# Two edits in a four-layer kernel: the order of the 64-row products in `pair_heads`, and the buffers of the gate tiles

## Chip, cores and metric

The kernel runs on one core of a Trainium2 chip. The metric is device time in microseconds (us). Before the change it is 3857.72 us, the median of 3 runs (3853.47 to 3861.3).

## What is computed

The input x has 2048 rows of 1024 fp32 values. Four layers follow one another; each projects its input with a wide weight matrix, mixes rows in two or three ways, gates the result, projects it back with a second matrix, adds the input and normalises. Layers 2 and 3 are the two that the first edit touches. Layer 2 has gated linear attention with 4 heads, 64 key channels and 128 value channels each, in chunks; layer 3 has retention of the same sizes in chunks of 128 rows. Cut to what matters, retention is

```python
scores = jnp.einsum('bnihd,bnjhd->bnhij', q, k) * dmat          # causal, inside a chunk
o_intra = jnp.einsum('bnhij,bnjhe->bnihe', scores, v)
chunk_state = jnp.einsum('bnjhd,hj,bnjhe->bnhde', k, w_state, v)
s_in = _chunk_scan(chunk_decay, chunk_state)                     # state entering each chunk
o_inter = jnp.einsum('bnihd,hi,bnhde->bnihe', q, w_inter, s_in)
return (o_intra + o_inter).reshape(B, S, H, dv)
```

and gated linear attention has the same five steps with a decay for each key channel in place of the fixed one. In all four layers part of the mixed values is multiplied by a gate of the form `h * sigmoid(h)` of one slice of the input projection.

## The kernel before

The 2048 rows are worked on in 4 blocks of 512; blocks go through the layers in pairs. In a block and layer the work is: the input projection, weight tile by weight tile (`in_a`, `in_b`, `in_b4`), with the mixing between the tiles; the gate (`gate_mix`); the output projection (`out_proj`). Every projection is done with both operands split into a high and a low part, three products for one, accumulated in one of four PSUM banks named `acc`. A second pool of four PSUM banks, `mm`, serves all other products and transposes. Each weight tile (512 KB) is loaded by a DMA on SyncE's queue into one of two buffers `wst`, rounded by ScalarE into `whi` (line 444) and its remainder taken by VectorE into `wlo` (line 313).

The source states the work in one order; a planner in the language's tile framework then places each instruction on its engine by readiness and rank, where rank follows the order in the source and `high_priority` raises it. So the order found in the trace need not be that of the source. The helpers record all work at a few lines: products at 322 (`mmul`), transposes at 325 (`tr`), VectorE products at 310 and 313, ScalarE at 299. The profile must therefore be read by tiles: `acc` for projections, `mm<-u` for the scores (key times query), `mm<-vb,t` for the state increments (transposed key times value), `mm<-vb,am` for masked scores times value, `mm<-t,u` for query times state.

`pair_heads` (line 1169) handles two heads of 64 key channels at once: head 0 lies on partitions 0 to 63, head 1 on 64 to 127. It is called twice, once for each pair of heads, in each block of layers 2 and 3. In the four chunks t of a block it forms

- the scores, for head 0 all four chunks, then for head 1: products over 64 rows;
- the masks (`masked`, VectorE, into the constant tiles `am`), the transposes of the keys (`trans4`) and the increments, products over 128 rows that write 64 partitions each;
- the states, on VectorE (`state_chain` in layer 2, lines 1188 to 1193 in layer 3);
- the outputs, head by head and chunk by chunk: a product over 128 rows (masked scores times value) that begins a sum, then one over 64 rows (query times state) that ends it;
- `finish` for each head: `rms_to_mix` (layer 2) or `groupnorm_to_mix` (layer 3).

In layer 2 the two calls are made from a hook after the first and the second weight tile of an `in_a`; in layer 3 they follow each other directly, and the four projections of the pool branch come next. A product of fp32 operands appears in the trace as two matmul instructions.

`gate_mix` (line 773) ends the input projection of every layer and block, 16 times in all. For each of four row tiles ScalarE computes tanh from an accumulator into a tile `g`, VectorE multiplies it with the accumulator, which is then free, and GpSimd multiplies the tile into `mix`. `g` comes from a tag with two buffers (line 254); `u` is a tag with 13 buffers of the same size, from which norm parameters, input loads and many temporary tiles come.

Of the kernel before, what the change touches and what calls it, by code (L numbers as in the profile page):

```python
# [226 lines left out]
class Build:  # L227
# [544 lines left out]

    def gate_mix(self, accs, c0, n=512, half=None):
        for t in range(4):
            g = self.g((128, n))
            self.gate(accs[t][:, 0:n], g, 0.5 if half is None else half[:, t:t + 1])
            m = self.mix[:, t * 1024 + c0:t * 1024 + c0 + n]
            self.tt(m, m, g, ALU.mult, self.nc.gpsimd)
# [389 lines left out]

    def pair_heads(self, g, qd, kd, S, em, finish, coef=None):

        ams = []
        for i in range(2):
            r = slice(64 * i, 64 * i + 64)
            ps = self.mm()
            for t in range(4):
                c = slice(t * 128, t * 128 + 128)
                self.mmul(ps[:, c], kd[r, c], qd[r, c])
            ams.append(self.masked(ps))
        kT = self.trans4(kd)
        inc = self.mm()  # L1180
        for t in range(4):
            for i in range(2):
                self.mmul(inc[64 * i:64 * i + 64, t * 128:t * 128 + 128], kT[:, t * 128 + 64 * i:t * 128 + 64 * i + 64], self.vb[:, t, 2 * g + i, 0:128])
        if coef is None:
            Ss = self.state_chain(S, inc, em)
        else:
            Ss, iv = self.t(), self.t()
            self.nc.vector.tensor_copy(Ss[:, 0:128], S)
            self.act(iv, inc, AF.Copy, scale=coef)
            for t in range(4):  # L1190
                c = slice(t * 128, t * 128 + 128)
                dst = Ss[:, t * 128 + 128:t * 128 + 256] if t < 3 else S
                self.stt(dst, Ss[:, c], coef, iv[:, c], ALU.mult, ALU.add)
        for i in range(2):
            r = slice(64 * i, 64 * i + 64)
            o = self.mm()
            for t in range(4):
                c = slice(t * 128, t * 128 + 128)
                self.mmul(o[:, c], ams[i][:, c], self.vb[:, t, 2 * g + i, 0:128], start=True, stop=False)
                self.mmul(o[:, c], qd[r, c], Ss[r, c], start=False, stop=True)  # L1200
            finish(o, 2 * g + i)


    def ret_tables(self, b, C, S):
# [546 lines left out]
```

## Time and profile before

| | before |
|---|---|
| median of 3 runs | 3857.72 us (3853.47 to 3861.3) |
| profiled execution | 3849.46 us, span 3847.7 us |
| granted TensorE clock, mean | 0.996 |
| TensorE busy | 3740.3 us, 97% |
| VectorE busy | 2755.3 us, 72% |
| ScalarE busy | 1774.8 us, 46% |
| GpSimd busy | 586.0 us, 15% |
| HBM read, written | 378.82 MB, 58.72 MB: 114 GB/s over the span |

A row of the profile gives the line, the engine, the operation, the tile written and the tiles read, the partitions and elements of a product (64*128 is 64 rows by 128 columns of weights) and a count; in brackets stands how long the engine was idle just before and what ended that. In the chain of waits, each piece is a start, a length and what filled it. TensorE's instructions are pipelined, so their durations overlap; what one costs is read from the distance between starts.

### The profile page before, as it was taken

What the parts mean: (1) busy time and instruction counts of PE and PEld (TensorE: products, weight loads), DVE (VectorE), ACT (ScalarE), POOL (GpSimd) and SP (SyncE); (2) the same over time, 40 slices, a digit from 0 to 9 for tenths busy, and PEclk for the clock granted to TensorE, in tenths of its full rate; (3) what the DMA queues carried; (4) which work ended last, traced back from release to release, by engine and by line L of the source; (5) the groups of instructions that cost most, each with busy time, mean ns of one, the idle gap of its engine ahead of it and who ended that gap; (6) DMA issues with size and microseconds to landing.
All of it is one profiled execution on the core that took longest, in us unless ns stands there. A gap on an engine that the chain in (4) does not pass through costs nothing.

```text
span 3847.7 us, 54577 instructions
## 1 busy us (share of the span) xinstructions
PE 3740.3 (97%) x20576; PEld 3119.7 (81%) x20576; DVE 2755.3 (72%) x5807; ACT 1774.8 (46%) x3273; POOL 586.0 (15%) x445
## 2 busy tenths in 40 slices
PE   8999999999999999999999999999999999999999
PEld 7788788878787878888787887888887878888887
DVE  7776765667666798598677767656676767985985
ACT  6547343434242454355374573434333424653552
POOL 0110112112121201100301101121131211012003
PEclk9999999999999999999999999999999999999999
DMA  3332343433343332321423332434343433223212
GB/s 128 123 126 92 111 143 119 154 109 133 131 148 120 122 109 66 126 88 66 135 81 127 121 120 77 144 130 149 115 150 113 148 115 127 77 72 131 88 61 88
DMA packets 141528, 441.09 MB, mean 115 GB/s; under 512 B 15696, under 2 KB 15824, under 8 KB 141264
## 3 DMA queue, kind: packets, MB, share of 16 engines
q1 hardware_dynamic: 141264, 437.60, 33.5%
q8 instruction: 162, 2.65, 0.3%
q14 instruction: 102, 0.84, 0.1%
HBM read 378.82 MB, written 58.72 MB: 114 GB/s over the span
## 4 chain that ended last, share of the span: by engine, by line
PE 75%; DVE 13%; ACT 4%; DMA 3%; issue 2%; POOL 2%; SPq 0%; ACTq 0%; POOLq 0%; DVEq 0%
PE acc L322 61%; PE mm L322 10%; PE mm L325 4%; DVE wlo L313 3%; DMA wst<-in_wi_dram 3%; DVE u L310 2%; DVE t L313 1%; ACT whi L444 1%; POOL mix L313 1%; ACT t L299 1%; DVE t L310 1%; POOL u L313 0%; DVE g L310 0%; DVE mix L310 0%; DVE big L310 0%
## 5 line engine op out<-in xcount | busy, mean ns | idle before, releaser
L322 PE MATMUL acc<-whi,ah 128*128 128x512 f32 (+3 forms) x3072 | 1174.9, 382 | 31.3 <-DVE g L310 15.0
L322 PE MATMUL acc<-wlo,ah 128*128 128x512 f32 (+3 forms) x3072 | 1164.1, 379 | 0.0
L322 PE MATMUL acc<-whi,al 128*128 128x512 f32 (+3 forms) x3072 | 1162.1, 378 | 0.0
L313 DVE TENSOR_TENSOR wlo<-wst,whi 128x1024 fp32r<-128x1024 f32 (+2 forms) x560 | 732.0, 1308 | 475.2 <-ACT whi L444 453.7
L444 ACT CAST whi<-wst 128x1024 fp32r<-128x1024 f32 (+2 forms) x560 | 573.9, 1025 | 965.9 <-PE acc L322 609.9
L322 PE MATMUL acc<-ah,whi 128*128 128x512 f32 (+1 forms) x2048 | 709.8, 347 | 9.1 <-ACT whi L444 9.1
L322 PEld LDWEIGHTS acc<-whi,ah 128*128 128x128 f32 x3072 | 579.3, 189 | 152.6 <-DVE g L310 23.1
L322 PE MATMUL acc<-ah,wlo 128*128 128x512 f32 (+1 forms) x2048 | 697.2, 340 | 0.5 <-DVE wlo L313 0.5
L322 PE MATMUL acc<-al,whi 128*128 128x512 f32 (+1 forms) x2048 | 697.0, 340 | 0.0
L322 PEld LDWEIGHTS acc<-whi,al 128*128 128x128 f32 x3072 | 578.9, 189 | 112.4
L322 PEld LDWEIGHTS acc<-wlo,ah 128*128 128x128 f32 x3072 | 579.9, 189 | 107.9 <-issue 1.0
L322 PEld LDWEIGHTS acc<-ah,whi 128*128 128x128 f32 x2048 | 387.1, 189 | 49.9 <-ACT whi L444 9.1
L322 PEld LDWEIGHTS acc<-ah,wlo 128*128 128x128 f32 x2048 | 386.5, 189 | 42.1 <-issue 1.4
L322 PEld LDWEIGHTS acc<-al,whi 128*128 128x128 f32 x2048 | 387.2, 189 | 41.2 <-issue 2.9
L313 POOL TENSOR_TENSOR big<-big,u 128x512 f32<-128x512 f32 x96 | 139.9, 1489 | 580.3 <-PE mm L325 236.7
L313 POOL TENSOR_TENSOR mix<-mix,g 128x512 f32<-128x512 f32 x88 | 115.5, 1324 | 588.0 <-DVE g L310 520.0
L310 DVE SCALAR_TENSOR_TENSOR u<-mix,hdw,u 128x512 f32<-128x512 f32 x240 | 170.7, 746 | 0.3
L538 ACT CAST ah<-u 128x512 fp32r<-128x512 f32 x128 | 79.2, 619 | 179.7 <-PE acc L322 167.6
L310 DVE SCALAR_TENSOR_TENSOR big<-big,acc 128x512 f32<-128x512 f32 x128 | 87.5, 683 | 77.8 <-PE acc L322 77.5
L313 POOL TENSOR_TENSOR u<-u,lc 128x512 f32<-128x512 f32 (+1 forms) x64 | 76.3, 1198 | 349.1 <-DVE u L319 172.0
L322 PE MATMUL mm<-t,u 64*128 64x128 f32 (+2 forms) x480 | 101.3, 308 | 14.5 <-DVE t L313 12.8
L310 DVE SCALAR_TENSOR_TENSOR g<-g,acc 128x512 f32<-128x512 f32 x112 | 76.0, 684 | 46.1 <-ACT g L299 46.1
(345 smaller groups left out, 4801.1 us busy)
## 6 DMA issues: line engine op xcount, KB each, us to landing
wst<-in_wi_dram SPq DMA_DIRECT2D x400, 512.0 KB, 3.3
wst<-in_wo_dram SPq DMA_DIRECT2D x128, 512.0 KB, 3.3
rows<-big SPq DMA_DIRECT2D x48, 512.0 KB, 2.7
chn<-t SPq DMA_DIRECT2D x96, 256.0 KB, 4.1
u<-chn SPq DMA_DIRECT2D x96, 256.0 KB, 4.8
big<-rows SPq DMA_DIRECT2D x48, 512.0 KB, 5.6
u<-in_lnp_dram SPq DMA_DIRECT2D x48, 256.0 KB, 5.2
u<-in_xt_dram SPq DMA_DIRECT2D x32, 256.0 KB, 4.2
```

What stands on the lines that cost most here:

```text
L299: return self.nc.scalar.activation(out, in_, f, bias=bias, scale=scale)
L310: return self.nc.vector.scalar_tensor_tensor(out, in0, s, in1, op0, op1)
L313: return (eng or self.nc.vector).tensor_tensor(out, a, b, op)
L322: return self.nc.tensor.matmul(out, lhsT, rhs, start=start, stop=stop)
L325: return self.nc.tensor.transpose(out, in_, self.ident)
L444: nc.scalar.copy(hi, st)
L538: nc.scalar.copy(h, c4(st))
```

## The change

The first edit is in `pair_heads`. The scores of both heads are formed together, chunk by chunk, head 0 and head 1 in turn, into two PSUM banks. The outputs of both heads are collected in two banks at once: first all products over 128 rows, then all products over 64 rows, again chunk by chunk with the heads in turn. Since the four chunks of a head share a bank and their sums are now open together, only the first product of a bank is marked as its start, and only the last as its end. `finish` is called for both heads after all products. The second edit is in `gate_mix`: the tiles of the third and fourth row tile come from `u` instead of `g`.

```diff
     def gate_mix(self, accs, c0, n=512, half=None):
         for t in range(4):
-            g = self.g((128, n))
+            g = self.g((128, n)) if t < 2 else self.u((128, n))
...
     def pair_heads(self, g, qd, kd, S, em, finish, coef=None):
 
-        ams = []
-        for i in range(2):
-            r = slice(64 * i, 64 * i + 64)
-            ps = self.mm()
-            for t in range(4):
-                c = slice(t * 128, t * 128 + 128)
+        rows = [slice(0, 64), slice(64, 128)]
+        pss = [self.mm() for _ in range(2)]
+
+        for t in range(4):
+            c = slice(t * 128, t * 128 + 128)
+            for ps, r in zip(pss, rows):
                 self.mmul(ps[:, c], kd[r, c], qd[r, c])
-            ams.append(self.masked(ps))
+        ams = [self.masked(ps) for ps in pss]
...
+        os = [self.mm() for _ in range(2)]
         for i in range(2):
-            r = slice(64 * i, 64 * i + 64)
-            o = self.mm()
             for t in range(4):
                 c = slice(t * 128, t * 128 + 128)
-                self.mmul(o[:, c], ams[i][:, c], self.vb[:, t, 2 * g + i, 0:128], start=True, stop=False)
-                self.mmul(o[:, c], qd[r, c], Ss[r, c], start=False, stop=True)
-            finish(o, 2 * g + i)
+                self.mmul(os[i][:, c], ams[i][:, c], self.vb[:, t, 2 * g + i, 0:128], start=(t == 0), stop=False)
+        for t in range(4):
+            c = slice(t * 128, t * 128 + 128)
+            for o, r in zip(os, rows):
+                self.mmul(o[:, c], qd[r, c], Ss[r, c], start=False, stop=(t == 3))
+        for i in range(2):
+            finish(os[i], 2 * g + i)
```

## Prediction

> **What bounds the kernel now.** I read the page first: busy time, then the chain of waits.
>
> ```profile
> span 3847.7 us, 54577 instructions
> PE 3740.3 (97%) x20576; PEld 3119.7 (81%) x20576; DVE 2755.3 (72%) x5807; ACT 1774.8 (46%) x3273; POOL 586.0 (15%) x445
> PE 75%; DVE 13%; ACT 4%; DMA 3%; issue 2%; POOL 2%; SPq 0%; ACTq 0%; POOLq 0%; DVEq 0%
> ```
>
> TensorE is the bound nearly everywhere: 97% busy, 75% of the chain. A busy TensorE need not be one at its peak, though, so the question is how densely its products stand where the change works. For that I took the chain of waits through the two calls of `pair_heads` in one block of layer 3 (970 to 1030 us).
>
> ```profile
> 981.22 1.64 PE mm L322 x16
> ...
> 984.36 8.32 PE mm L322 x64
> ...
> 995.40 6.67 PE mm L322 x44
> ...
> 1002.31 0.42 PE mm L322 x4
> 1002.73 24.92 PE acc L322 x106
> ```
>
> Every piece here is TensorE, so a microsecond taken from its products in this stage comes off the end, as long as nothing else becomes late. How they stand is seen in the timeline of TensorE (start, duration, shape, count). Each fp32 product of 128 columns is two matmul instructions, so a call has 16 for the scores (`mm<-u`, 64 rows), 16 for the state increments (`mm<-vb,t`), 16 for the masked scores times v (`mm<-vb,am`, 128 rows) and 16 for q times state (`mm<-t,u`, 64 rows).
>
> ```profile
> 981.15 1.71 PE L322 MATMUL mm<-u 64*128 64x128 f32 x16
> 982.79 0.66 PE L325 MATMUL mm<-ident,u 128*128 128x128 f32 x4
> ...
> 984.29 1.09 PE L322 MATMUL mm<-vb,t 128*64 128x128 f32 x16
> 985.32 0.49 PE L322 MATMUL mm<-vb,am 128*128 128x128 f32 x2
> 985.74 0.48 PE L322 MATMUL mm<-t,u 64*128 64x128 f32 x2
> 986.15 0.71 PE L322 MATMUL mm<-vb,am 128*128 128x128 f32 x4
> 986.79 0.49 PE L322 MATMUL mm<-t,u 64*128 64x128 f32 x2
> ```
>
> Two instructions of one shape take 0.42 us from their start to the start of the other shape (985.32 to 985.74, 985.74 to 986.15); four take 0.64 (986.15 to 986.79). So each further instruction of the same shape costs 0.11, and a change of shape costs 0.42 - 2 x 0.11 = 0.20. The present order changes shape after every product. A second view shows two halves of the partitions meeting, at the end of the first call: its last product reads rows 64 to 127, the next call's scores begin on rows 0 to 63.
>
> ```profile
> 990.55 0.49 PE L322 MATMUL mm<-vb,am 128*128 128x128 f32 x2
> 990.97 0.37 PE L322 MATMUL mm<-t,u 64*128 64x128 f32 x1
> 990.97 0.37 PE L322 MATMUL mm<-u 64*128 64x128 f32 x1
> 991.18 0.27 PE L322 MATMUL mm<-t,u 64*128 64x128 f32 x1
> 991.19 1.50 PE L322 MATMUL mm<-u 64*128 64x128 f32 x15
> 992.61 0.51 PE L322 MATMUL acc<-al,whi 128*128 128x512 f32 x1
> ```
>
> The two start together at 990.97 and go on together at 991.18 and 991.19: products on different halves overlap fully.
>
> **The change part by part.** No product, copy or DMA is added or removed. Calls: the groups of instructions by shape give the count, and 256 / 16 = 16 calls (2 groups, 2 layers, 4 blocks).
>
> ```profile
> L322 PE MATMUL mm<-t,u 64*128 64x128 f32 x256 | 54.5, 322 | 0.0
> ```
>
> *128-row and 64-row products apart.* Before, in this call: 985.32 to 990.97 for 30 of the 32, 5.65 us, and 0.1 for the last two, which overlap the next call: 5.75. In layer 2 products of the input projection stand between, and the chain shows the same density, 0.188 us for one instruction:
>
> ```profile
> 568.21 3.75 PE mm L322 x20
> ```
>
> ```profile
> 566.51 0.56 DVE L313 TENSOR_TENSOR t<-t,em 128x384 f32<-128x384 f32 x1
> ```
>
> I take 5.8 for both. After: 16 of 128 rows in one stretch are 0.42 + 14 x 0.11 = 1.96; 16 of 64 rows, eight on each half side by side, are 0.42 + 6 x 0.11 = 1.08. Together 3.04, so 2.75 is saved in a call of layer 3. In layer 2 the states of the last three chunks come from one VectorE product (566.51 to 567.07, the row above) and the first chunk's earlier, so the 64-row stretch will break once: 0.2 more, 2.55 saved.
>
> *Scores alternating.* Before, 981.15 to 982.79: 1.64 us. They already overlap in part: 16 in series would be 0.42 + 14 x 0.11 = 1.96. After, as above, 1.08: 0.56 saved. That alternation in this very pattern keeps both halves going is borne out by the increments, which alternate halves of the columns: 984.29 to 985.32 is 1.03 us for 16. If the halves did not overlap at all, the scores would lose 0.32 and q times state would be 1.96, so a call gains 5.8 - 3.92 - 0.32 = 1.56, 25 us over 16 calls. This is the lower end, and 8 x (2.75 + 0.56) + 8 x (2.55 + 0.56) = 51 us is what I take, since the row at 990.97 is the same operation. Without any break in layer 2 it is 53, the upper end.
>
> *Both results at the end of a call.* The normalisation of the first head used to begin while the second head's products ran; now both begin after the last product. In layer 3 VectorE is in order, and behind the normalisation stand the masks of the second call, for which its 128-row products wait.
>
> ```profile
> 989.82 0.89 DVE L1293 BATCH_NORM_STATS2 st<-mm 128x6 f32<-128x128 f32 x4 [2.08 <-PE mm L322]
> ...
> 997.91 1.36 DVE L319 TENSOR_SCALAR mix<-mm,mv,y 128x128 f32<-128x128 f32 x4
> ```
>
> ```profile
> 981.00:1002.70 21.70, 21.70 (x152) 16.41 (x151) 13.46 (x58) 4.08 (x6) 0.00 (x0) 1.00 0.12 37
> 1002.70:1028.00 25.30, 25.30 (x111) 20.20 (x109) 24.72 (x76) 6.70 (x9) 7.15 (x4) 1.00 0.28 91
> ```
>
> These are the two windows' busy times (length, PE, PEld, DVE, ACT, POOL, clock, DMA). VectorE has 13.46 us of work in a stage that shrinks from 21.7 to about 15: it fits, with little to spare. TensorE has cover for the second call's wait: the four projections for the pool branch, each 24 products of about 0.235 (106 in 24.92 us), need only free accumulators. I charge 0.75 us for each of the 4 blocks of layer 3, 3 us in all, for places where the written order does not match; the ends are 0 and the 29 us of the rival below. In layer 2 a whole weight tile's products stand between the two calls; nothing is charged.
>
> *Gate tiles.* With two buffers, ScalarE's third gate waits until GpSimd has multiplied the first into the mix. The last block of layer 4 shows the dearest case:
>
> ```profile
> 3787.53 5.93 POOL L313 TENSOR_TENSOR mix<-mix,y 128x512 f32<-128x512 f32 x4 [3.33 <-DVE y L313]
> 3793.42 2.49 POOL L313 TENSOR_TENSOR mix<-mix,g 128x512 f32<-128x512 f32 x2
> ```
>
> ```profile
> 3794.72 0.69 ACT L299 ACTIVATE g<-acc,rs 128x512 f32<-128x512 f32 x1 [4.90 <-POOL mix L313]
> ```
>
> ```profile
> 3796.19 0.80 PE L322 MATMUL acc<-whi,ah 128*128 128x512 f32 x1 [2.13 <-DVE g L310]
> ```
>
> ```profile
> 3796.20:3804.00 7.80, 7.80 (x27) 6.17 (x28) 3.64 (x3) 2.42 (x3) 2.52 (x2) 0.79 0.21 67
> ```
>
> GpSimd's normalisation (to 3793.46) holds up its gate products, ScalarE stands 4.90 us, and the output projection waits 2.13 us for the accumulator; after that its granted clock is 0.79 for 7.8 us, 7.8 x 0.21 = 1.6 us more. With a buffer for each gate the third needs only its accumulator: 3.7 us here. Elsewhere less:
>
> ```profile
> 1868.40 0.50 PE L322 MATMUL acc<-whi,ah 128*128 128x512 f32 x1 [1.24 <-DVE g L310]
> 1869.63 0.50 PE L322 MATMUL acc<-whi,ah 128*128 128x512 f32 x1 [0.26 <-DVE g L310]
> ...
> 885.27 0.50 PE L322 MATMUL acc<-whi,ah 128*128 128x512 f32 x1 [0.30 <-DVE g L310]
> ```
>
> That is 1.5 in the second block of layer 4, and at most 0.3 in each of the other 14: 1.8 as my estimate, since most show less. Together 7 us. The upper bound is what TensorE waits for gates at all, the lower nothing:
>
> ```profile
>   PEld acc L322: 23.1, 18
> ```
>
> Of those 23.1 us the longest are waits for the *first* gate, which no buffer shortens, so I put the upper end at 10. The two tiles that now come from `u` (13 buffers) are free again after a GpSimd product of about 1.25 us (2.49 for two), at the head of an output projection of four weight tiles and more. Behind them in the order of `u` are at most four tiles of norm parameters and eight of the next input, 14 with the two: only the last input load can meet one, and then it is long free. Nothing is charged; without that cover an input load would land late by as much as it waits, 1.25 us. Nothing is moved past a DMA: neither edit issues one, and the queues of SP and POOL keep their order.
>
> **Sum.** -51 (products) + 3 (second calls) - 7 (gates) = -55 us. The profiled execution took 3849.46 us, 1.76 more than its span; 3849.46 - 55 = 3794.5. The median of the runs, 3857.72, is 1.00215 times the profiled one, so the forecast for a median is 3794.5 x 1.00215 = 3802.6, say 3802. Its own range: gains from 25 + 0 - 3 = 22 to 53 + 10 = 63, thus 3795 to 3836.
>
> **Rivals.** *A, the wait in layer 3 takes the gain back.* If TensorE's order puts the second call's transposes ahead of the pool projections, it stands while VectorE normalises both heads. VectorE's work from 989.82 to 999.27 (rows above) is 9.45 us; TensorE has only the next scores, 1.64, and the transposes, 0.6 (the row at 982.79), to set against it: 7.2 us idle, 29 in four blocks. The gain is 51 + 7 - 29 = 29, the median 3829. For it: VectorE's 24.72 of 25.3 us busy right after the calls. Against it: the present order already lays projection products there (992.61). The Trainium skill, "TensorEngine Tiling (Array Packing)", "Restrictions and Gotchas", speaks for this side: row tiling raises the pressure on PSUM, since different row tiles write to different banks; here both results hold a bank until both are normalised. No run here shows yet what that costs. Chance 0.13.
>
> *B, the planner keeps the products mixed.* The order on the engine is not that of the source: before, `mm<-t,u` already stands between `mm<-vb,am`. If readiness still decides, masks against states, only the scores (9 us) and the gates (7) gain: 3842. Against it: the 128-row products of both heads now come first in the source, the states later, so both rank and readiness keep them apart. Chance 0.07.
>
> *C, slower: each alternation is itself a change of shape.* If going from one half to the other drained the array as going from 128 to 64 rows does, each product of two instructions would cost 0.42: scores 8 x 0.42 = 3.36 instead of 1.64, q times state 3.36 and the 128-row stretch 1.96 instead of 5.8 together. A call would lose 1.72 - 0.48 = 1.24, 20 us in all, with the gates 13: 3871. It decides from the price at which a product of two instructions costs 0.37: 16 x 0.37 + 1.96 = 7.9, against 5.8 + 1.64 + 7/16. Against it: 990.97, where the halves meet at no price, and the increments. Chance 0.04.
>
> *D, no change,* from small losses in a new plan of the whole program that eat the gain: every product's place follows from the planner, and the change touches layers 2 and 3 only but moves the rest. Nothing in the profile gives such a loss a place; 0.03 within, 0.01 for slower.
>
> **How the numbers follow.** The forecast gets 0.72, A 0.13, B 0.07, C 0.04, D 0.04. About 0.2% (8 us) is what a measurement of this kernel can tell from no change. Faster by more: 0.72 + 0.13 + 0.07 = 0.92; same 0.03; slower 0.05. The range is the forecast's own, 3795 to 3836, which holds A's 3829 too; at the low end I add the spread of the runs, 4 us to each side of their median, and one more: 3790 to 3836. B, C and D are left out, 0.15, and little of the forecast.
>
> **What would show each step.** In the changed profile: stretches `mm<-vb,am` x16 (or x8 twice) and `mm<-t,u` x16 with starts 0.11 apart on two halves; 1.1 us from the scores to the transposes instead of 1.64; about 3 us for masked scores and states instead of 5.8; the layer 3 stage of 21.7 us at about 15; no ScalarE wait for GpSimd's `mix` at a gate, and no clock of 0.79 after 3796. The forecast is wrong if alternating halves keep a spacing of 0.2 or more, if TensorE waits for a mask or a state in the second calls of layer 3, or if the stages shrink as said and as much reappears as waits for weights at the next layer's start.

## The result, and the profile after

| | before | after |
|---|---|---|
| median of the runs | 3856.8 us (3853.47 to 3861.3) | 3788.15 us (3785.87 to 3790.02) |
| profiled execution | 3849.46 us, span 3847.7 us | 3785.87 us, span 3784.2 us |

The median of before is that of four runs now, the forecast had three of them. The ratio is 0.9821, with an interval of 0.9804 to 0.9838: 68.65 us less by the medians, 63.6 by the two profiled executions. The forecast was 3802 us, in a range of 3790 to 3836. The kernel is faster, as expected, but by more than the range allowed.

The page of the changed kernel, the busy times and the shares of the chain:

```profile
PE 3684.2 (97%) x20576; PEld 3089.8 (82%) x20576; DVE 2740.5 (72%) x5807; ACT 1772.7 (47%) x3273; POOL 587.5 (16%) x445
PE 75%; DVE 14%; ACT 5%; DMA 3%; issue 3%; POOL 1%; SPq 0%; ACTq 0%; POOLq 0%; DVEq 0%
```

The counts of the engines are those of before; TensorE is busy 56 us less and bounds as much of the chain as it did. In the timeline of TensorE (start, duration, shape, count), the first call in the same block of layer 3, and the start of the second:

```profile
970.03 1.16 PE L322 MATMUL mm<-u 64*128 64x128 f32 x16
971.12 0.65 PE L325 MATMUL mm<-ident,u 128*128 128x128 f32 x4
...
972.64 1.09 PE L322 MATMUL mm<-vb,t 128*64 128x128 f32 x16
973.72 2.02 PE L322 MATMUL mm<-vb,am 128*128 128x128 f32 x16
975.67 1.16 PE L322 MATMUL mm<-t,u 64*128 64x128 f32 x16
976.67 1.06 PE L322 MATMUL mm<-u 64*128 64x128 f32 x16
...
980.20 0.66 PE L325 MATMUL mm<-ident,u 128*128 128x128 f32 x4 [0.17 <-DVE nq L313]
```

From start to start the scores take 1.09 us (1.64 before), the 128-row products 1.95 in one stretch, query times state 1.00. The forecast had 1.08, 1.96 and 1.08. The second call's transposes wait 0.17 us; its 64-row stretch breaks into 12 and 4 instructions, which the forecast had in layer 2 alone. The whole stage, both calls and the projection products between them (window, length, then busy times):

```profile
970.03:986.42 16.39, 16.22 (x155) 13.23 (x155) 13.27 (x58) 4.08 (x6) 0.00 (x0) 1.00 0.16 49
```

Before, the stage ran from 981.15 to 1002.66, 21.51 us, with 14 projection products inside; now there are 18. At 0.235 us each the four more make 0.94, so 16.39 - 0.94 = 15.45 us stand against 21.51: 6.06 less for two calls, where the forecast had "at about 15". In layer 2 (timeline of TensorE, first call):

```profile
560.45 1.16 PE L322 MATMUL mm<-u 64*128 64x128 f32 x16
...
563.30 1.09 PE L322 MATMUL mm<-vb,t 128*64 128x128 f32 x16 [0.19 <-ACT t L759]
564.81 2.02 PE L322 MATMUL mm<-vb,am 128*128 128x128 f32 x16 [0.42 <-DVE am L751]
566.76 0.49 PE L322 MATMUL mm<-t,u 64*128 64x128 f32 x4
568.11 0.94 PE L322 MATMUL mm<-t,u 64*128 64x128 f32 x12
```

The 64-row stretch breaks once, as foretold. New are the waits in brackets: TensorE stands 0.19 us for ScalarE's copy of the transposes and 0.42 us for the masks.

Who waits for a gate tile `g` (us, times), the answer to the row "23.1, 18" of before:

```profile
  PEld acc L322: 5.4, 4
```

and the four places of layer 4 in the timeline of TensorE, at the start of the output projection:

```profile
1531.20 0.50 PE L322 MATMUL acc<-whi,ah 128*128 128x512 f32 x1 [1.28 <-DVE g L310]
...
1835.93 0.50 PE L322 MATMUL acc<-whi,ah 128*128 128x512 f32 x1 [0.51 <-DVE g L310]
...
3428.08 0.50 PE L322 MATMUL acc<-whi,ah 128*128 128x512 f32 x1 [1.35 <-DVE g L310]
...
3732.98 0.50 PE L322 MATMUL acc<-whi,ah 128*128 128x512 f32 x1 [0.52 <-DVE g L310]
```

The first two of these were, before:

```profile
1556.82 0.78 PE L322 MATMUL acc<-whi,ah 128*128 128x512 f32 x1 [3.89 <-DVE g L310]
...
1865.51 0.50 PE L322 MATMUL acc<-whi,ah 128*128 128x512 f32 x1 [2.51 <-DVE g L310]
```

All of these are waits for the first gate of a block. The waits for the third and fourth are gone, and three of the first ones are shorter than before (3.89, 2.51 and, in the third block, 3.90 us then; the 0.52 of the last was 0.51), which the forecast had excluded. ScalarE's waits for GpSimd's `mix` ahead of a tile `g` fall from 50.0 us in 38 to 7.5 in 8.

To place the gain I compared the starts of the same projection products in the two traces. The gain grows by 22.2 us in the four blocks of layer 2 and 23.6 in those of layer 3, at the calls of `pair_heads`: 45.8 for the products. It grows by 4.9, 4.0, 4.5 and 3.8 us at the four gates of layer 4: 17.2. Everything else nets 0.6. The products came out near the forecast's 48; the gates brought 17.2 where it had 7. Of the 17.2, 5.1 are stretches at half clock that stood behind three of these gates in the profile of before and are gone; 12 are waits.

### The profile page after: what moved, and what is told of

Its sections match the earlier page's. It is cut to its first block, busy times and chain, and to the rows that moved or that the text cites. A ratio compares the mean times of both kernels' runs of the same rounds, so it can differ in the third digit from the quotient of the medians.

```text
span 3784.2 us, 54674 instructions
## 1 busy us (share of the span) xinstructions
PE 3684.2 (97%) x20576; PEld 3089.8 (82%) x20576; DVE 2740.5 (72%) x5807; ACT 1772.7 (47%) x3273; POOL 587.5 (16%) x445
## 4 chain that ended last, share of the span: by engine, by line
PE 75%; DVE 14%; ACT 5%; DMA 3%; issue 3%; POOL 1%; SPq 0%; ACTq 0%; POOLq 0%; DVEq 0%
PE acc L322 62%; PE mm L322 9%; PE mm L325 4%; DVE wlo L313 3%; DMA wst<-in_wi_dram 3%; DVE u L310 2%; DVE t L313 1%; ACT whi L444 1%; ACT t L299 1%; DVE t L310 1%; POOL u L313 0%; DVE mix L310 0%; DVE u L313 0%; POOL mix L313 0%; DVE t L1011 0%
## 5 line engine op out<-in xcount | busy, mean ns | idle before, releaser
L322 PE MATMUL acc<-whi,ah 128*128 128x512 f32 (+3 forms) x3072 | 1172.0, 381 | 20.9 <-DVE u L313 11.6
L322 PEld LDWEIGHTS acc<-whi,ah 128*128 128x128 f32 x3072 | 579.2, 189 | 136.5 <-ACT t L300 10.2
L313 POOL TENSOR_TENSOR mix<-mix,g 128x512 f32<-128x512 f32 x56 | 78.6, 1414 | 580.9 <-DVE g L310 513.6
L299 ACT ACTIVATE t<-mm,cols 128x128 f32<-128x128 f32 (+2 forms) x272 | 98.3, 489 | 16.1 <-PE mm L322 11.1
L322 PE MATMUL mm<-big,u 128*128 128x256 f32 (+2 forms) x616 | 94.9, 289 | 6.3 <-DVE u L313 6.3
```

What stands on the lines that cost most here:

```text
L299: return self.nc.scalar.activation(out, in_, f, bias=bias, scale=scale)
L313: return (eng or self.nc.vector).tensor_tensor(out, a, b, op)
L322: return self.nc.tensor.matmul(out, lhsT, rhs, start=start, stop=stop)
```

## The experiments

Medians in us. Each row is measured beside runs of the kernel before on the same chip: 3854.12 for the first four, 3853.11 for the next four, 3852.51 for e9 to e11, 3853.11 for e12. The last column is the loss to half clock in the one profiled execution: the windows at half clock in its records, times one half. The last window of every trace is counted whole though it reaches past the last instruction, so each figure is 1.0 us too high, and no difference between rows is touched by that. It is one execution's figure; the medians come from all of them.

| run | median | against before | ratio, interval | half clock |
|---|---|---|---|---|
| e1_gates | 3834.53 | -19.6 | 0.9950, 0.9936 to 0.9963 | 12.4 |
| e2_products | 3812.0 | -42.1 | 0.9887, 0.9874 to 0.9901 | 25.0 |
| e3_series | 3798.39 | -55.7 | 0.9855, 0.9841 to 0.9868 | 13.0 |
| e5_own_tag | 3845.36 | -8.8 | 0.9977, 0.9968 to 0.9986 | 18.8 |
| e6_lc_early | 3851.43 | -1.7 | 0.9996, 0.9986 to 1.0006 | 14.9 |
| e7_tag_lc | 3833.98 | -19.1 | 0.9956, 0.9939 to 0.9972 | 8.7 |
| e4_gates4 | 3833.38 | -19.7 | 0.9952, 0.9936 to 0.9968 | 11.7 |
| e8_before_again | 3854.70 | one execution | | 19.8 |
| e9_scores | 3851.87 | -0.6 | 0.9999, 0.9990 to 1.0008 | 14.9 |
| e10_by_head | 3809.81 | -42.7 | 0.9889, 0.9874 to 0.9905 | 12.1 |
| e11_after_lc | 3791.01 | -61.5 | 0.9837, 0.9823 to 0.9850 | 12.1 |
| e12_scores_alone | 3855.70 | +2.6 | 1.0003, 0.9994 to 1.0011 | 25.1 |

The first profile of before lost 14.9 us to half clock, the profile of after 11.5.

### Each edit alone: e1_gates and e2_products

e2 has `pair_heads` as after and the gate tiles of before; e1 is the kernel before with

```diff
-            g = self.g((128, n))
+            g = self.g((128, n)) if t < 2 else self.u((128, n))
```

> The kernel before with the second edit alone: the third and fourth gate tile from `u`. The order written for the engines differs from before in two ways that the forecast didn't expect: SyncE's queue issues the next block's input loads behind weight tiles instead of between them, and at the end of layer 4 VectorE does the other blocks' work (`lc`, `u<-vpv,u`) earlier or later than the gates instead of right ahead of them. Theory O (order): in layer 4 the first gate comes earlier too, and the gain is that of the four layer 4 stages of the two traces, 4.9 + 4.0 + 4.5 + 3.8 = 17.2, and about 1.5 elsewhere: 16 to 20 us below before. The forecast's step F: only the third and fourth gate gain, 7 us, at most 10.

> The kernel before with the first edit alone: `pair_heads` as changed, gate tiles from `g`. The two traces give 22.2 us in the four layer 2 stages and 23.6 in the four layer 3 stages, 45.8: I expect 44 to 50 us below before. The forecast said 51 - 3 = 48. If it were about 60, the gates would be right as forecast and the products mis-sized; if below 40, the two edits would not add up to the whole.

The gates alone bring 19.6 us, as theory O said and nearly three times the forecast's term. The products alone bring 42.1 by the median. In its profiled execution e2 gains 47 us at the calls of `pair_heads` but loses 10 us more to half clock than the profile of before did (25.0 against 14.9), so its span falls only by 35.8. The two edits sum to 61.7, the whole is 66 to 69: they add up within what the measurements can tell. (The 47 us are counted from a few products ahead of each call; counted so, the kernel after gains 47 there as well.)

### What in the gate edit brings the gain: e5, e6, e7, e4

The written order of e1 differs from before on two engines; the forecast had said "the queues of SP and POOL keep their order" and had nothing on VectorE. SyncE's queue in the first block of layer 4, before (start, duration, transfer, count):

```profile
1543.03 0.33 SPq L720 DMA_DIRECT2D lc<-in_lc_dram  x1
1544.12 0.33 SPq L441 DMA_DIRECT2D wst<-in_wo_dram  x1
1544.49 1.62 SPq L535 DMA_DIRECT2D u<-chn  x3
```

and after (e1 has the same order):

```profile
1520.02 0.33 SPq L720 DMA_DIRECT2D lc<-in_lc_dram  x1
1521.11 8.61 SPq L441 DMA_DIRECT2D wst<-in_wo_dram  x3
1529.76 1.85 SPq L535 DMA_DIRECT2D u<-chn  x4
```

Two tiles of `u` are taken by gates, so the next block's input loads, which also need `u`, are written later. VectorE's order changes as well: at three of the four gates of layer 4, work of other blocks (`lc<-lc,cols`; in the second block `u<-vpv,u`) is moved relative to the gates. Three experiments take this apart.

In e5, on the kernel before, the gates have their own buffers, but not from `u`:

```diff
-            g = self.g((128, n))
+            g = self.g((128, n)) if t < 2 else self.pw()[:, 0:n]
```

> The kernel before, but the third and fourth gate tile come from the tag `pw` (three buffers, used only by the band of layer 4, idle at the gates) instead of `u`. Each gate tile has a buffer as in the change, but the written order of TensorE, VectorE and SyncE's queue stays that of before, apart from the names of these tiles. Theory O: the first gates stay as late as before, so only the waits for the third and fourth gate go: 3.8 in the last block of layer 4, some 1.9 in its second, 2 elsewhere, 6 to 10 us below before. Rival B (the buffer itself brings all of it): 17 to 20 us below before.

e6, on the kernel before, changes `lconst` alone, and e7 has both edits:

```diff
-                self.ts(near[:, h], near[:, h], self.col("relc", h), None, ALU.subtract)
+                with self.hp(): self.ts(near[:, h], near[:, h], self.col("relc", h), None, ALU.subtract)
```

> The kernel before with one edit only: VectorE's four subtractions `lc<-lc,cols` (the next block's layer 4 table) get a raised priority. Gate tiles stay two buffers of `g`. On VectorE the four stand earlier by a few rows in two blocks of layer 4, ahead of the last step of a normalisation that starts GpSimd; on the other engines nothing changes. Theory O: the first gate of these two blocks comes earlier, TensorE's stall there goes from 4.1 us to about 1.5, and with it a window or two of half clock (1.7 us each): 6 to 12 us below before, though no gate has a new buffer. Rival B (the stall depends on the gate buffers): 0, within 3 us of before.

> Own buffers for the third and fourth gate from `pw` and the earlier `lc<-lc,cols`, both on the kernel before; SyncE's queue as before. Theory O: both parts add, 8.8 and 6 to 12, so 15 to 20 us below before, about the 19.6 of the second edit alone; what is left is the second block's first gate (2.7 us, `u<-vpv,u` stands ahead of it), which should stay. If the new order of the input loads on SyncE's queue is what brings the gain, it stays at 9.

e4, on the kernel before, takes `u` in layer 4 alone, the only caller that passes `half`:

```diff
-            g = self.g((128, n))
+            g = self.g((128, n)) if t < 2 or half is None else self.u((128, n))
```

> The kernel before with gate tiles from `u` in layer 4 only. If layer 4 carries the gain of the second edit, 17 to 20 us below before, like the 19.6 of the edit in all layers. The forecast's term gave layer 4 little more than 5.2 and the rest under 1.8: about 6.

Own buffers in the old order bring 8.8 us, the forecast's 7 within the interval (5 to 12); at the four gates of the profiled execution they bring 7.6. TensorE's waits for gates in e5, in all, count and longest, and the first two of them in its timeline:

```profile
PEld acc L322 <- DVE g L310: 11.7, 4, 4.3
```

```profile
1559.49 0.52 PE L322 MATMUL acc<-whi,ah 128*128 128x512 f32 x1 [3.89 <-DVE g L310]
...
1867.75 0.50 PE L322 MATMUL acc<-whi,ah 128*128 128x512 f32 x1 [2.51 <-DVE g L310]
```

Four waits instead of 18: the third and fourth gates no longer hold anything, the four first gates do, as long as before but for the third block's (3.05 us, 3.90 before). The earlier `lc` alone (e6) gives 1.7 us, inside its noise, and not the 6 to 12 that I expected. The third block of layer 4 shows why, first in a second profile of before (below), then in e6:

```profile
3490.37 0.50 PE L322 MATMUL acc<-whi,ah 128*128 128x512 f32 x1 [3.90 <-DVE g L310]
3493.24 0.79 PE L322 MATMUL acc<-whi,ah 128*128 128x512 f32 x1 [0.56 <-DVE g L310]
```

```profile
3487.71 0.50 PE L322 MATMUL acc<-whi,ah 128*128 128x512 f32 x1 [1.70 <-DVE g L310]
3491.49 0.50 PE L322 MATMUL acc<-whi,ah 128*128 128x512 f32 x1 [2.10 <-DVE g L310]
```

The wait for the first gate is 2.2 us shorter, but the next one, for the third gate, grows from 0.56 to 2.10: with two buffers ScalarE's third gate stands for GpSimd (3.46 us here), whose normalisation now starts behind `lc` and a `wlo` and runs right up to its gate products. In the first block the first wait falls from 3.89 to 2.69 and the next one rises from 0.56 to 1.22; VectorE there stands 1.38 us for ScalarE's `whi` before it reaches the gate. In the second block, where no `lc` stands, both waits stay. Both edits together (e7) bring 19.1 us, more than 8.8 and 1.7:

```profile
PEld acc L322 <- DVE g L310: 8.1, 4, 2.9
```

So the two waits stand one behind the other in front of the same accumulators. Removing the first alone only shifts the time to the second; removing the second alone leaves the first. But this is the smaller part of the excess. By the starts of the projection products around the four gates, with the loss to half clock taken off, TensorE gains 5.9 us on the first profile of before in e5, 1.3 in e6, 9.2 in e7 and 11.8 in e1 (on the second profile about 1 us less in each): together the two edits are worth 2 us more than one by one. The rest is clock and the scatter of the runs. Behind the four gates the six profiles with two gate buffers (before, e2, e6, e8, e9, e12) lose 5.1 to 10.2 us to half clock, e5 loses 3.4, and the seven with more buffers and earlier first gates (after, e1, e3, e4, e7, e10, e11) lose nothing.

In e7 SyncE's order is that of before, so the new order of the input loads is not needed for the gain; VectorE's order is. And e4, with `u` in layer 4 alone, gets the 19.7 of the whole edit: the gates of layers 1 to 3 bring nothing that can be measured.

How a few small rows on VectorE can delay the first gate is seen in the timeline of VectorE, before:

```profile
1548.84 2.06 DVE L313 TENSOR_TENSOR wlo<-wst,whi 128x1024 fp32r<-128x1024 f32 x1
1550.83 2.17 DVE L318 TENSOR_SCALAR lc<-lc,cols 128x256 f32<-128x256 f32 x2
1552.92 2.06 DVE L313 TENSOR_TENSOR wlo<-wst,whi 128x1024 fp32r<-128x1024 f32 x1
1554.90 1.27 DVE L310 SCALAR_TENSOR_TENSOR al<-mm,ah 128x512 fp32r<-128x512 f32 x2
1556.10 1.27 DVE L310 SCALAR_TENSOR_TENSOR g<-g,acc 128x512 f32<-128x512 f32 x2
```

and after:

```profile
1525.80 1.22 DVE L313 TENSOR_TENSOR wlo<-wst,whi 128x1024 fp32r<-128x1024 f32 x1
1527.03 0.35 DVE L318 TENSOR_SCALAR lc<-lc,cols 128x256 f32<-128x256 f32 x1
1527.50 1.85 DVE L313 TENSOR_TENSOR wlo<-wst,whi 128x1024 fp32r<-128x1024 f32 x1
1529.28 1.28 DVE L310 SCALAR_TENSOR_TENSOR al<-mm,ah 128x512 fp32r<-128x512 f32 x2
1530.48 1.27 DVE L310 SCALAR_TENSOR_TENSOR g<-g,acc 128x512 f32<-128x512 f32 x2
```

From the first `wlo` to the gate it is 7.26 us before and 4.68 after. The same `wlo` takes 2.06 and 1.22, an `lc` 1.08 and 0.35. GpSimd's timeline shows the difference, before and after:

```profile
1548.74 5.15 POOL L313 TENSOR_TENSOR mix<-mix,y 128x512 f32<-128x512 f32 x4 [3.50 <-DVE y L313]
```

```profile
1527.19 5.06 POOL L313 TENSOR_TENSOR mix<-mix,y 128x512 f32<-128x512 f32 x4 [4.96 <-DVE y L313]
```

Before, GpSimd's normalisation starts ahead of the first four of these VectorE instructions and they run at its side; after, VectorE does three `lc` and one `wlo` first and only then the last step of `y` that lets GpSimd start. Seen one by one, the instructions of before take turns: GpSimd's first runs to 1549.82, the `wlo` that began 0.1 us behind it to 1550.90; GpSimd's second, from 1549.79, takes 2.02 us instead of 1.08 and ends 0.9 behind the `wlo`; the first `lc` ends 0.14 behind that. So here each of the two engines stands for a whole instruction of the other. The Trainium skill, "SBUF — State Buffer", section "SBUF: two separate sides", says that a pair of ports is shared by GpSimd and by VectorE instructions of some kinds, such as those with two inputs in SBUF (`wlo` is one), and that whichever starts first has it for the whole instruction; the trace agrees in the turns (2.06 us for a `wlo`, 2.02 for GpSimd's product). No run here shows which port it is.

### The clock: e8_before_again

> The kernel before once more, for a second profile. The first profiled execution took 3849.46 us, 15 runs beside the experiments have a median of 3854.12. If the gap comes from the clock, the stalls of TensorE at layer 4's output projections are the same within 0.3 us, and the loss by windows of half clock differs from the 14.9 us of the first profile by about what the time differs from 3849.46. If it comes from stalls, these are longer and the windows the same.

It took 3854.70 us, 5.2 more than the first profiled execution, and lost 19.8 us to half clock instead of 14.9: 4.9 more. The first-gate waits are those of before to 0.1 us. Windows behind the gates of layer 4, first and second block, in the first profile of before (the third figure from the right is the granted clock):

```profile
1556.80:1564.00 7.20, 7.17 (x22) 5.05 (x23) 4.17 (x4) 2.31 (x3) 5.04 (x4) 0.76 0.17 66
1865.00:1873.00 8.00, 5.99 (x24) 4.28 (x25) 4.66 (x5) 2.31 (x3) 5.07 (x4) 1.00 0.21 76
```

and in the second:

```profile
1559.00:1566.20 7.20, 6.64 (x17) 4.66 (x16) 3.57 (x3) 2.31 (x3) 4.53 (x4) 0.53 0.14 43
1869.60:1877.00 7.40, 6.50 (x18) 4.49 (x17) 3.58 (x3) 2.31 (x3) 4.17 (x4) 0.54 0.15 48
```

In the first block the same first wait is followed once by 3.4 us at half clock (7.2 x 0.24 x 2) and once by 6.8 (7.2 x 0.47 x 2), in the second once by none and once by 6.8. The Trainium skill, "TensorE: Matmul & The Clock Gate", section "What's actually happening", describes a free-running window of 3413 ns that decides; the trace agrees in the length, 3.4 us or a multiple of it for every slow stretch behind a gate. That the window runs freely would explain why the same wait falls differently; no run here sets its phase. With the loss taken off the span, three profiles of before agree far better than their times: 3832.8, 3833.2 and 3834.3 us (e9 is the third). On that footing e1 is 11.6 us below the first profile, e2 45.9, after 60.1. So the gates' 19.6 by the medians is about 12 of waits and, by subtraction, about 8 of clock and scatter: in e1 none of the four gates of layer 4 is followed by half clock, in each of the three profiles of before three are, at 1.7 or 3.4 us.

### The products taken apart: e3, e10, e12

In e3, on the kernel after, the two loops change places in the scores and in query times state, here the latter:

```diff
-        for t in range(4):
-            c = slice(t * 128, t * 128 + 128)
-            for o, r in zip(os, rows):
+        for o, r in zip(os, rows):
+            for t in range(4):
+                c = slice(t * 128, t * 128 + 128)
                 self.mmul(o[:, c], qd[r, c], Ss[r, c], start=False, stop=(t == 3))
```

> The kernel after, but within the scores and within query times state the heads come one after the other instead of in turn; 128-row and 64-row products stay apart. Theory H (halves overlap when they alternate): the scores go back to 1.64 us from 1.09 and query times state takes as much, so 2 x 0.55 = 1.1 us a call is lost, 17.6 us over 16 calls: about 51 us below before. Rival S (only the separation of shapes matters): nothing is lost, 68 us below before. Rival P (the heads in series don't overlap at all): 2 x (1.96 - 1.09) x 16 = 28 us lost, 40 below before.

In e10, on the kernel after, this stands in place of all that follows the states:

```diff
+        for i, r in enumerate(rows):
+            o = self.mm()
+            for t in range(4):
+                c = slice(t * 128, t * 128 + 128)
+                self.mmul(o[:, c], ams[i][:, c], self.vb[:, t, 2 * g + i, 0:128], start=(t == 0), stop=False)
+            for t in range(4):
+                c = slice(t * 128, t * 128 + 128)
+                self.mmul(o[:, c], qd[r, c], Ss[r, c], start=False, stop=(t == 3))
+            finish(o, 2 * g + i)
```

> The kernel after with the outputs written head by head: eight instructions over 128 rows, then eight over 64 rows, `finish`, then the other head. Scores and gates as after. This is the forecast's rival B put to the test: written so, the planner's order on TensorE is mixed again, in layer 3 128-row and 64-row products change six more times a call, in layer 2 twice more. At 0.20 us a change that is 8 x 1.2 + 8 x 0.4 = 12.8 us, and up to 0.8 us a call for the lost alternation of halves: 13 to 26 us above after. If only the count of products mattered, it would be the same as after; if the earlier `finish` of the first head were worth something, below after.

e9 and e12 were to hold the new scores alone, on the kernel before:

```diff
-        for i in range(2):
-            r = slice(64 * i, 64 * i + 64)
-            ps = self.mm()
-            for t in range(4):
-                c = slice(t * 128, t * 128 + 128)
+        for t in range(4):
+            c = slice(t * 128, t * 128 + 128)
+            for ps, r in zip(pss, rows):
                 self.mmul(ps[:, c], kd[r, c], qd[r, c])
```

> The kernel before with the scores alone as changed: both heads in turn; outputs and gates stay. The forecast gave this 0.56 us in each of 16 calls, 9 us; the changed kernel's profile shows 1.09 instead of 1.64, the same. Expected: 7 to 11 us below before, and with the 42.1 of the whole first edit 31 to 35 are left for the outputs. If the masks now come too late or the planner moves other work, it is under 5.

> The kernel before with the scores alone as changed: in both calls the eight products of the two heads in turn; outputs and gates stay. (The run named e9_scores held the kernel before without this edit and is no test of it.) The forecast gave the scores 0.56 us in each of 16 calls, 9 us; the changed kernel's profile shows 1.09 instead of 1.64, the same. Expected: 7 to 11 us below before, so that of the 42.1 of the whole first edit 31 to 35 are left for the outputs. If the masks now come too late for the outputs, or the next call's scores lose the overlap that they had with the last product of the call before, it is under 5.

e3 loses 10.2 us against after by the medians, 10.7 between the profiled spans and 13 by the differences to before, so halves in turn do matter (rival S falls), but less than 17.6. By the starts of the projection products a stage of two calls loses 1.5 us in layer 3 and 0.8 to 0.95 in layer 2, instead of 2.2 in each. In layer 3 the timeline shows a reason at the seam of two calls:

```profile
978.16 1.37 PE L322 MATMUL mm<-t,u 64*128 64x128 f32 x13
979.27 0.37 PE L322 MATMUL mm<-u 64*128 64x128 f32 x1
979.38 0.27 PE L322 MATMUL mm<-t,u 64*128 64x128 f32 x1
```

Head 1's products with the state (rows 64 to 127) overlap with the next call's scores of head 0 (rows 0 to 63): the halves find each other anyway, where two stretches on different halves follow one another. In layer 2 no calls meet; there the first call has nothing to lose in the scores, since in the kernel after it stands for the copy and the masks (0.19 and 0.42 us), and e3 doesn't.

e10 costs 21.7 us against after by the medians and 24.7 between the profiled spans, within the 13 to 26 expected. Written head by head, the order on TensorE is mixed again (timeline, first call in layer 3):

```profile
980.27 1.13 PE L322 MATMUL mm<-vb,am 128*128 128x128 f32 x8
981.33 0.48 PE L322 MATMUL mm<-t,u 64*128 64x128 f32 x2
981.74 0.49 PE L322 MATMUL mm<-vb,am 128*128 128x128 f32 x2
```

A product of two instructions takes 0.41 us from shape to shape, as before. So the planner does mix where the source lets it (the forecast's rival B); that the changed source puts all 128-row products of both heads first is what holds them apart. e10 differs from after in the loss to half clock by 0.6 us only, so the 24.7 are products.

In e9 the edit was missing: it is the kernel before, and its 0.9999 is a measure of what no change looks like. e12 has the edit and no gain: 1.0003, where I expected 7 to 11 us less. The scores do take 1.09 us (561.19 to 562.28), but in the first call of layer 2 the time returns two rows later (timeline of TensorE in e12):

```profile
564.05 1.09 PE L322 MATMUL mm<-vb,t 128*64 128x128 f32 x16 [0.19 <-ACT t L759]
565.56 1.00 PE L322 MATMUL mm<-vb,am 128*128 128x128 f32 x4 [0.41 <-DVE am L751]
```

TensorE reaches the increments earlier and stands for the copy and then for the masks. Before, VectorE masks the first head's scores ahead of a `wlo` and the second's behind it; with the heads in turn both masks stand behind that `wlo`, in e12 as in the kernel after. So from the first score to the masked products it is 4.37 us in this call and 4.17 before; the second call keeps its gain. From the first score to the projection product behind the last 64-row one, two calls take 26.86 us in this block instead of 27.21, and about 0.3 less in each of the eight stages: 2.6 us in all. The interval of the ratio goes from 2.3 us less to 4.2 more, so such a gain lies at its edge; the profiled execution lost 25.1 us to half clock, where the three of before lost 14.9 to 19.8.

### Can it be better: e11_after_lc

The kernel after, with the edit of e6.

> The kernel after, with the raised priority for `lc<-lc,cols`. On VectorE the four subtractions and one `wlo` come ahead of the normalisation's last steps in two blocks of layer 4. TensorE's wait for the first gate is 1.46 and 1.54 us there in the kernel after; if VectorE's queue ahead of the gate still sets it, it falls to about 1 and the time by 0 to 3 us; if the later start of GpSimd's normalisation delays the hand-over to the output projection, it is up to 2 us longer.

3791.01 us, ratio 0.9837 (0.9823 to 0.9850), against 0.9821 (0.9804 to 0.9838) of after: not told apart. What order could give at these gates, the edit itself already gives.

## Why the prediction was wrong in size

**TensorE bounds these stages, and shape changes are the cost: right.** Each price came out: 1.09, 1.95 and 1.00 us against 1.08, 1.96 and 1.08, the break in layer 2 included. Rival C (a halves' change drains) is excluded by the same rows.

**Products, -51 + 3: right in the sum, 45.8, not in its parts.** The separation of outputs brings about 43 (45.8 less the 2.6 of e12, if the two add; forecast 42.4). The scores were put at 9 us and brought 2.6 in e12: in layer 2's first calls ScalarE's copy and VectorE's masks end the wait, in layer 3's a state does (0.16 us in e12's first block). For such waits the forecast charged 3 us to layer 3's second calls and nothing to layer 2; the one in layer 3 is 0.17 us, and those in layer 2 took the whole gain of the first calls. So it is luck that the sum is so near: two errors, 6 and 3 us, partly cancel. Rival A did not happen: the second call's wait in layer 3 is 0.17 us, not 7.2. The rule on the pressure on PSUM, for which the Trainium skill was cited there ("TensorEngine Tiling (Array Packing)", "Restrictions and Gotchas"), has no larger price than that here.

**Gates, -7: the step that failed.** "Of those 23.1 us the longest are waits for the *first* gate, which no buffer shortens, so I put the upper end at 10", and "the queues of SP and POOL keep their order". Taken as a buffer and nothing else, the term is right: e5 has 8.8. But the change takes the tiles from `u`, other work needs `u`, and the planner writes another order for VectorE, in which the first gates of three blocks come 2 to 2.6 us earlier (waits of 3.89 and 2.51 in the first two, of which 1.28 and 0.51 are left). Together the waits fall from 23.1 to 5.4 us. Half of the waits' gain is the buffers' (5.9 us in e5) and half the order's (11.8 in e1). The clock was under-counted too: the forecast charged half clock at one gate (1.6 us), each profile of before has it at three (5.1 to 10.2 us), and after has it at none.

**The factor 1.00215: also wrong.** It carried the gap between the median and the profiled execution of before over to after. But this gap is not a property of a kernel: the profiled execution had been a lucky one (14.9 us lost to half clock; the next had 19.8), while after's median is 1.0006 times its profiled time. Of the 14 us between 3802 and 3788.15, about 10 are the gates, 6 the factor, and the products' 2 count the other way. The range failed for the same two reasons: its largest gain, 63, was nearly that of the two profiled executions (63.6), but made of 53 and 10 where 45.8 and 17.2 were measured; and with after's own factor, 1.0006, its low end would have been 3784 instead of 3790.

**Left open.** Why the planner moves VectorE's rows when the tiles come from `u` is not shown, only that it does (e1 against e5). The second block's `u<-vpv,u` was not moved by itself; that it explains the 2.51 us there (0.51 after) rests on its place in the order and on e7, where it stays ahead of the gate and TensorE's wait is still 2.50. With that wait e7 should stay some 2 us behind e1; its median does not (19.1 and 19.6), which their intervals can't decide. And how often half clock follows a given wait is known here from a few profiles only.

## What to carry to other kernels

Ask of a buffer change from which pool the tiles come and who else draws on it: where a planner writes the order, a buffer taken from a shared tag can move loads and fillers on other engines, and here this was worth as much in waits (6 us) as the buffer itself. Two waits in front of the same resource don't add: taking away the first alone gave nothing in one block (e6), so test them together; and look at the clock before the excess is called waits. A gain on the engine that bounds a stage only counts up to the next result it needs: 0.55 us faster scores gave 0.16 a call.

## What the runs showed of the hardware that was not expected

- A wait of TensorE of 2.51 us and one or two more soon after (0.90, or 1.24 and 0.26) were followed by 6.8 us at half clock in one execution and by none in another of the same kernel. Between these two the loss differs by 4.9 us (14.9 against 19.8), and e2 and e12 lost 25. A wait of 2.5 us with no second one behind it (second block in e5 and e7) was followed by none, one of 3.05 and one of 3.89 (e5) by 3.4 us each.
- VectorE's `wlo` of 128x1024 took 1.22 us alone and 2.06 in turns with GpSimd's normalisation, an `lc` of 128x256 0.35 and 1.08, and GpSimd's product 1.08 and 2.02. `al<-mm,ah`, which reads PSUM, took 0.68 us beside the same normalisation in e7 and 0.68 behind it in before.
- Two 64-row products on different halves overlap also across the seam of two unrelated stretches, as in e3: no alternation in the source is needed there.
